# Carrying transposed gate/up blocks through DRAM, with a re-planned instruction order, in a macaron block with an RWKV-7 and pooling mixer

## The chip, the core and the metric

The kernel runs on one core of one Trainium2 chip. The metric is the time of one execution on the device in microseconds, the median of several runs. A core has five engines that run side by side, each working through its own instructions in order: TensorE (PE in the profile; its weight loads are PEld), VectorE (DVE), ScalarE (ACT), GpSimd (POOL) and SyncE (SP). SP computes nothing here; it issues most of the DMA transfers. An instruction whose inputs are not ready holds up everything behind it on its own engine, and this is true of SP's queue of transfers too.

## The reference

One block over 256 tokens of width 2048, in float32: a half-weighted SwiGLU feed-forward (FFN) of inner width 5632, a mixer, and a second such FFN.

```python
def _swiglu(x, w_gate, w_up, w_down):
    return (jax.nn.silu(x @ w_gate) * (x @ w_up)) @ w_down
...
def reference(x, ...):
    h = x
    for l in range(DEPTH):
        f = _swiglu(_rmsnorm(h, ln_ffn1_pre[l]), ffn1_gate[l], ffn1_up[l], ffn1_down[l])
        h = h + MACARON_WEIGHT * _rmsnorm(f, ln_ffn1_post[l])
        mx = _hybrid_mixer(_rmsnorm(h, ln_mix_pre[l]), ...)
        h = h + _rmsnorm(mx, ln_mix_post[l])
        f = _swiglu(_rmsnorm(h, ln_ffn2_pre[l]), ffn2_gate[l], ffn2_up[l], ffn2_down[l])
        h = h + MACARON_WEIGHT * _rmsnorm(f, ln_ffn2_post[l])
    return h
```

DEPTH is 1. The mixer multiplies by `w_in`, runs an RWKV-7 scan over 16 heads and a pooling branch, gates the two, and multiplies by `w_out`. The change concerns the hidden activations of the two FFNs, `silu(x @ w_gate) * (x @ w_up)`, on their way to the product with `w_down`, and the order of all instructions.

## The kernel before

**Products.** Every float32 matrix is split into a high part H (cast to fp32r) and a low part L (the rest), and a product is three passes on TensorE: H·H, H·L, L·H (`mm3`, line 510). Weights come from DRAM by SP into one of five raw buffers `w32` of 128x1024 floats (`raw`, line 466; 512 KB, which is two k of 128 rows by 512 columns). ACT casts a raw buffer to `wH`, VectorE subtracts to give `wL` (`split`, line 491); there are five buffers of each of these too (`WS_BUFS`). In the profile raw buffers are named w. A raw buffer is free for the next load when VectorE has made `wL`.

**FFN.** The inner width is worked through in 11 blocks of 512 columns (`ffn`, line 846). A block takes the gate columns (bank names f0, f1, for the two halves of 128 tokens) and the up columns (l0, l1), over 16 k of 128. Pairs of k may instead be done by a seven-product scheme (`early` and `late`, lines 732 and 751), called quads here: four products of a quad run within the block before (early), three in its own block (late). A quad takes its weights as six half loads into three raw buffers, and VectorE forms sums of them first. `GATE_QUADS` gives the quads of a block: none in blocks 0 and 1, three in 2 to 8, two in 9 and 10. `block_seq` (line 819) lays out a block: gate pairs with late quads between, then up pairs, with the next block's early quads put in at even distances.

**From a block to the down product.** At a block's end the activations lie with tokens on the partitions, but the down product wants the inner columns there. VectorE transposes 32x32 squares within the partitions into a tile `T1` (`turn`, line 659; named T in the profile). What is left is to exchange 32-partition groups, since a transpose of 128x128 moves the square (i, q) to (q, i). `carry` (line 664) does this by 16 DMA transfers on SP from `T1` to another tile `x32` (named x), each 32 partitions by 256 columns, 32 KB. Then ACT casts x to a high part and VectorE subtracts for the low part, two halves each (named xH, xL); they are `hT`, which the down product reads only after all 11 blocks. There are two FFNs, so 22 carries and 352 such transfers.

**Mixer and stage borders.** `gemm_tok` with `lead` (line 516) is used for the first product after a norm (mixer and second FFN): it loads `STAG` k of weights and does the first half of the tokens for these before the second half, so that TensorE has work while the second half is still being normalised and transposed. With `trail` it does the last 16 k of a stage half by half (`by_half`, line 550); there the weights of the first `STAG` k use the five rotating buffers, and those of the rest are held in units, the pool of 33 tiles of 128x1024 floats (`NUNITS`) which all activations share.

**What sets the order.** Nothing is issued directly. Every call is recorded as an `Op`, and `Plan` works out the order for all engines by simulating them (`simulate`, line 237), then emits it (`emit`, line 369). Since `emit` makes all instructions at line 391, the profile gives L391 for every one of them, and groups are told apart by the tiles' names. Planned costs come from `cost` (line 185): a transfer occupies SP's queue for 370 ns, and moves at 387 GB/s or less for short rows. In the simulation a transfer's data moves no earlier than 1900 ns after its issue and after the transfers before it; it counts as landed 300 ns after that. `deadlines` (line 218) gives each op a due time from its users, a DMA 2000 ns earlier; of the ready ops of an engine, the one due first goes first. An op off TensorE may be taken only when its nominal time is at most `AHEAD` ns, 25,000, past where TensorE's main stream stands. On the chip each engine keeps the planned order, whatever the real times are, and waits where the inputs of the next one aren't there.

Of the kernel before, what the change touches and what calls it, by code (L numbers as in the profile page):

```python
# [19 lines left out]
P = 128  # L20
# [15 lines left out]
W32_BUFS = 5  # L36
WS_BUFS = 5
NUNITS = 33
STAG = 10
TRAIL = 16  # L40
WARM = 12
TB = 6
AHEAD = 25000.0
EASE = 2.0
GATE_QUADS = [0, 0] + [3] * 7 + [2, 2]
DOWN_QUADS = ((8, 1, 2.4), (8, 1, 1.7))
# [17 lines left out]
class Engine:  # L64

    def __init__(s, plan, key, real):
        s.plan, s.key, s.real = plan, key, real
# [4 lines left out]


SYNC = 55.0
TABLES = {AF.Exp: (0,), AF.Sigmoid: (2,), AF.Tanh: (0, 2, 18), AF.Silu: (18,)}
IN_ORDER = ("w32", "wH", "wL", "hH", "hL")


class Plan:
# [105 lines left out]
    def cost(s, o, name, w, r, k):  # L185
        psum = any(getattr(s.tiles.get(x.tensor.name), "psum", False) for x in w + r)
        size = lambda ap: math.prod(ap.shape[1:]) if len(ap.shape) > 1 else 1
        n = max([size(x) for x in w + r] or [0])
        o.tab, o.nbytes = None, 0
        if name == "dma_start":  # L190
            x = w[0]
            o.nbytes = math.prod(x.shape) * 4
            run = min(min(y.shape[-1] for y in w + r) * 4, 2048)
            o.dur = o.nbytes / (387.0 if run >= 2048 else 387.0 * max(run, 64) * 1.25
                                / (run + 512))
            o.pace = {"SP": 370.0, "ACT": 110.0, "POOL": 600.0}[o.eng]
            return
        if o.eng == "PE":
            c = size(w[0])
            slow = name == "matmul" and r[0].dtype == F32  # L200
            o.pace = 2 * (0.7 * c + 32) / 2.4 if slow else (c + 32) / 2.4
            o.dur = o.pace + 165
        elif o.eng == "ACT":
            extra = 90.0 * sum(isinstance(k.get(x), bass.AP) for x in ("scale", "bias"))
            extra += 100.0 if "accum_out" in k else 0.0
            o.tab = TABLES.get(k.get("func"))
            o.pace, o.dur = n / 1.2 + 103 + extra, n / 1.2 + 200 + extra
        elif o.eng == "DVE":
            f = 1 / 0.96
            if name in ("tensor_copy", "tensor_scalar") and not psum:  # L210
                f /= 2
            more = 45.0 if name == "scalar_tensor_tensor" else 26.0 if name == "transpose" \
                else 0.0
            o.pace, o.dur = n * f + 75 + more, n * f + 158 + more
        else:
            o.pace = o.dur = n * 1.0 + 110

    def deadlines(s):
        for o in s.ops:
            for p in o.preds:  # L220
                s.ops[p].succs.append(o)
        soon = {}
        for o in s.ops:
            if o.stream == "chain":
                soon[o.i] = max([soon[q] + s.ops[q].dur + SYNC for q in o.preds if q in soon
                                 and s.ops[q].nom == o.nom] or [0.0])
        for o in reversed(s.ops):
            d = o.nom + (0.0 if o.eng == "PE" else o.lag) + soon.get(o.i, 0.0) * EASE
            for x in o.succs:
                if o.eng == "PE" and x.eng == "PE":  # L230
                    continue
                e = x.dl - o.dur - SYNC - (2000 if o.nbytes else 0)
                if e < d:
                    d = e
            o.dl = d

    def simulate(s):
# [18 lines left out]
        events, now, done, dma, tab = [], 0.0, 0, 0.0, None  # L256
        out, rel = [], itertools.count()
# [11 lines left out]
        def go(o):  # L269
            nonlocal done, dma, tab, prog  # L270
            e = o.eng
            if o.stream == "main" and e == "PE":
                prog = o.nom
            o.start = now
            for i in o.new:
                if i.slot is None:
                    i.slot = slots[i.tag].popleft()
                    turn[i.tag] += 1
            pace, dur = o.pace, o.dur
            if o.tab and tab not in o.tab:  # L280
                tab = o.tab[0]
                pace, dur = pace + 1300, dur + 1300
            free[e] = now + pace
            if o.nbytes:
                dma = max(now + 1900, dma) + o.dur
                o.end = dma + 300
            else:
                o.end = now + dur
            done += 1
            out.append(o)  # L290
            heapq.heappush(events, (free[e], next(rel), None))
            for i in o.tiles:
                i.left -= 1
                i.dl = max(getattr(i, "dl", 0.0), o.end)
                if not i.left and i.tag in s.tags:
                    heapq.heappush(events, (i.dl + SYNC, next(rel), i))
            for x in o.succs:
                t = now if e == "PE" and x.eng == "PE" else o.end + SYNC
                if x.stream == "chain" and x.eng == "PE" and e != "PE":
                    t += 250  # L300
                x.ready = max(x.ready, t)
                x.left -= 1
                if not x.left:
                    heapq.heappush(wait[x.eng], (x.ready, x.i))
                    heapq.heappush(events, (x.ready, next(rel), None))
        while done < len(ops):
            moved = True
            while moved:
                moved = False
                for e in engines:  # L310
# [3 lines left out]
                    while w and w[0][0] <= now:  # L314
                        _, i = heapq.heappop(w)
# [3 lines left out]
                    g = gate[e]  # L319
                    while g and g[0][0] <= prog + AHEAD:  # L320
                        i = heapq.heappop(g)[1]
                        heapq.heappush(av, (ops[i].dl, i))
                    if e == "PE":
                        for st in rank:
                            q = streams[st]
                            if q and ready[q[0].i] and can(q[0]):
                                go(q.popleft())
                                moved = True
                                break
                        continue  # L330
                    skipped = []
                    while av:
                        d, i = heapq.heappop(av)
                        if can(ops[i]):
                            go(ops[i])
                            moved = True
                            break
                        skipped.append((d, i))
# [8 lines left out]
            while events and events[0][0] <= now:  # L347
                _, _, i = heapq.heappop(events)
# [56 lines left out]
class Block:  # L405
    def __init__(s, tc, ctx):
        s.tc = tc
        s.real = real = tc.nc
        E = ctx.enter_context
        s.n = 0  # L410
        s.after = []
        s.cp = E(tc.tile_pool(name="cp", bufs=1))
        s.wp = E(tc.tile_pool(name="wp", bufs=1))
        s.up = E(tc.tile_pool(name="up", bufs=1))
        s.tp = E(tc.tile_pool(name="tp", bufs=1))
        s.sp = E(tc.tile_pool(name="sp", bufs=1))
        s.dp = E(tc.tile_pool(name="dp", bufs=1, space=bass.MemoryType.DRAM))
        s.pm = E(tc.tile_pool(name="pm", bufs=1, space=PSUM))
        s.pt = E(tc.tile_pool(name="pt", bufs=1, space=PSUM))
        s.nc = s.plan = Plan(tc)  # L420
        s.ident = s.const([P, P], "ident")
        make_identity(real, s.ident)
        s.mhalf = s.const([P, 16], "mhalf")
        real.gpsimd.memset(s.mhalf, -0.5)
# [91 lines left out]
    def gemm_tok(s, w, c0, at, KT, evac, lead=False, trail=False, xs=None):  # L516
# [11 lines left out]
        def both(k0, k1):  # L528
            for k2 in range(k0, k1, 2):
                keep(s.load_w(w, k2, min(2, k1 - k2), c0, 512))  # L530
                for k in range(k2, min(k2 + 2, k1)):
                    do(k, 0)
                    do(k, 1)
# [9 lines left out]
        elif lead:  # L543
            s.by_half(w, c0, 0, STAG, do, keep)
            k0 = STAG
        both(k0, KT)
# [3 lines left out]
    def by_half(s, w, c0, k0, k1, do, keep, done=None):  # L550
        for k in range(k0, k1, 2):
            keep(s.load_w(w, k, 2, c0, 512, k - k0 >= STAG))
        for h in range(2):
# [110 lines left out]
    def carry(s, T1, T):  # L664
        nc = s.nc
        x = s.unit((P, 1024), F32, "x32")
        for i in range(4):
            for q in range(4):
                nc.sync.dma_start(out=x[q * 32:q * 32 + 32, i * 256:i * 256 + 256],
                                  in_=T1[i * 32:i * 32 + 32, q * 256:q * 256 + 256])  # L670
        v = x.rearrange("p (i h k t) -> p k h i t", i=4, h=2, k=4)
        T.extend(s.new_T(1))
        for h in range(2):
            H, L = [t.rearrange("p k (h i t) -> p k h i t", h=2, i=4)[:, :, h] for t in T[-1]]
            s.split(v[:, :, h], H, L)
# [1099 lines left out]
```

## Time and profile before

| | us |
|---|---|
| median of 3 runs (lowest, highest) | 2149.8 (2149.71, 2152.92) |
| the profiled execution, its own time | 2155.24 |
| its span, first to last instruction | 2153.5 |
| VectorE / ScalarE busy | 1669.6 / 1141.9 |
| queue 1 (SP's transfers), share of 16 DMA engines | 60.4% |
| mean traffic over the span | 207 GB/s |

The stages of the span: the first FFN's gate and up blocks until about 520 us, its down product until 755, the mixer until about 1413, the second FFN from there, with its down product from about 1915.

How to read it: times are microseconds from the first instruction, unless marked ns. Engine names with a q (SPq) mean an engine's queue of issued transfers. A group `out<-in` names tiles with their buffer numbers left out. A timeline row gives start, duration, engine, line, operation, tiles, a count of merged instructions, and in brackets the idle time of the engine before it with what ended it. TensorE is pipelined: a product of 512 columns is shown as 0.39 us long, but the next starts 0.227 us later when nothing holds it up, so its busy share overstates its use. A row of waits gives engine and tile, what it waited for, the sum, the count and the longest. A row of windows gives the stretch and its length, and the busy time of each engine with its instruction count.

### The profile page before, as it was taken

Reading aid. Unit: us, or ns where it says so; the run is one execution under the profiler, and the core shown is the slowest. Engines: PE = TensorE matmul, PEld = TensorE weight load, DVE = VectorE, ACT = ScalarE, POOL = GpSimd, SP = SyncE. Lnnn points to the kernel's source line nnn. Section 1 sums busy time; section 2 is a strip of 40 time slices with the busy share of each in tenths; the row PEclk is TensorE's granted clock in tenths of the full one; section 3 lists DMA queues with packets and bytes.
Section 4 is the critical chain, followed back from the end, with each engine's and each line's share of the span. In section 5 each row is a group of like instructions: output and inputs, shape, how many; then the busy total and the mean of one; then the engine's idle time right before and its main releaser. Section 6 shows DMA issues by size and latency. Waiting matters only on the chain.

```text
span 2153.5 us, 30194 instructions
## 1 busy us (share of the span) xinstructions
PE 2076.4 (96%) x10847; PEld 1724.4 (80%) x10847; DVE 1669.6 (78%) x2176; ACT 1141.9 (53%) x1520; POOL 74.8 (3%) x146
## 2 busy tenths in 40 slices
PE   9899999999999999999999999999999999999998
PEld 7777777788778889978987788877777777878786
DVE  7888878777979765798768756588887887679795
ACT  7555555554546564664556344465554564455453
POOL 1000000000000020001200110010000000000000
PEclk9999999999999999999999999999999999999999
DMA  7666677766657566536465475566666776666574
GB/s 265 195 225 226 203 239 243 233 218 195 213 190 265 200 208 199 152 112 207 121 210 159 138 254 182 189 207 222 226 212 227 244 244 218 203 208 214 194 260 141
DMA packets 258047, 444.85 MB, mean 207 GB/s; under 512 B 23007, under 2 KB 70249, under 8 KB 257897
## 3 DMA queue, kind: packets, MB, share of 16 engines
q1 hardware_dynamic: 251721, 422.47, 60.4%
q0 software_dynamic: 5888, 19.93, 2.7%
q8 instruction: 85, 1.39, 0.3%
q10 hardware_dynamic: 288, 0.52, 0.1%
q14 instruction: 65, 0.53, 0.1%
HBM read 422.91 MB, written 8.39 MB: 200 GB/s over the span
## 4 chain that ended last, share of the span: by engine, by line
PE 47%; DVE 18%; issue 12%; SPq 11%; DMA 8%; ACT 3%; POOL 0%; DVEq 0%; ACTq 0%; POOLq 0%
PE l L391 14%; SPq L391 11%; PE f L391 9%; PE mm L391 9%; DVE wL L391 9%; PE mc L391 8%; DMA w<-in_ffn_gate_dram 5%; PE p L391 3%; ACT wH L391 2%; DVE t L391 2%; DVE w L391 1%; DVE sg L391 1%; DMA w<-in_ffn_up_dram 1%; DMA w<-in_ffn_down_dram 1%; DVE pr L391 1%
## 5 line engine op out<-in xcount | busy, mean ns | idle before, releaser
L391 ACT CAST wH<-w 128x1024 fp32r<-128x1024 f32 (+2 forms) x725 | 748.4, 1044 | 666.3 <-DVE w L391 158.8
L391 DVE TENSOR_TENSOR wL<-w,wH 128x1024 fp32r<-128x1024 f32 (+2 forms) x725 | 867.4, 1207 | 233.1 <-ACT wH L391 230.8
L391 PE MATMUL l<-wL,xH 128*128 128x512 f32 x772 | 303.9, 394 | 12.2 <-DVE wL L391 12.2
L391 PE MATMUL l<-wH,xH 128*128 128x512 f32 x772 | 303.3, 393 | 10.8 <-ACT wH L391 10.8
L391 PE MATMUL l<-wH,xL 128*128 128x512 f32 x772 | 301.7, 391 | 0.0
L391 PE MATMUL f<-wL,xH 128*128 128x512 f32 x664 | 261.2, 393 | 14.8 <-DVE wL L391 14.8
L391 PE MATMUL f<-wH,xH 128*128 128x512 f32 x664 | 260.1, 392 | 1.3 <-ACT wH L391 1.3
L391 PE MATMUL f<-wH,xL 128*128 128x512 f32 x664 | 259.7, 391 | 0.0
L391 PE MATMUL mm<-wL,xH 128*128 128x512 f32 x500 | 198.7, 397 | 3.0 <-DVE wL L391 3.0
L391 PE MATMUL mm<-wH,xH 128*128 128x512 f32 x500 | 197.3, 395 | 0.0
L391 PE MATMUL mm<-wH,xL 128*128 128x512 f32 x500 | 197.2, 394 | 0.0
L391 PEld LDWEIGHTS l<-wL,xH 128*128 128x128 f32 x772 | 145.6, 189 | 47.5 <-DVE wL L391 17.9
L391 PEld LDWEIGHTS l<-wH,xH 128*128 128x128 f32 x772 | 145.7, 189 | 47.0 <-ACT wH L391 17.1
L391 DVE TENSOR_TENSOR t<-w,w 128x1024 f32<-128x1024 f32 (+1 forms) x132 | 134.5, 1019 | 53.0 <-DMA w<-in_ffn_gate_dram 34.6
L391 PEld LDWEIGHTS l<-wH,xL 128*128 128x128 f32 x772 | 145.8, 189 | 29.6
L391 PEld LDWEIGHTS f<-wL,xH 128*128 128x128 f32 x664 | 125.5, 189 | 45.7 <-DVE wL L391 19.8
L391 PE MATMUL mc<-xH,wL 128*128 128x256 f32 x560 | 159.3, 284 | 1.1 <-DVE wL L391 1.1
L391 PE MATMUL mc<-xL,wH 128*128 128x256 f32 x560 | 159.8, 285 | 0.0
L391 PE MATMUL mc<-xH,wH 128*128 128x256 f32 x560 | 159.0, 284 | 0.0
L391 PEld LDWEIGHTS f<-wH,xH 128*128 128x128 f32 x664 | 125.5, 189 | 29.6 <-ACT wH L391 3.0
L391 PEld LDWEIGHTS f<-wH,xL 128*128 128x128 f32 x664 | 125.4, 189 | 25.7
L391 PEld LDWEIGHTS mm<-wL,xH 128*128 128x128 f32 x500 | 94.5, 189 | 23.8 <-DVE wL L391 4.3
(320 smaller groups left out, 3090.5 us busy)
## 6 DMA issues: line engine op xcount, KB each, us to landing
w<-in_w_in_dram SPq DMA_DIRECT2D x128, 512.0 KB, 3.9
w<-in_ffn_up_dram SPq DMA_DIRECT2D x126, 512.0 KB, 4.7
w<-in_ffn_gate_dram SPq DMA_DIRECT2D x124, 512.0 KB, 4.5
w<-in_ffn_down_dram SPq DMA_DIRECT2D x112, 512.0 KB, 4.8
w<-in_ffn_gate_dram SPq DMA_DIRECT2D x154, 256.0 KB, 4.2
w<-in_ffn_up_dram SPq DMA_DIRECT2D x150, 256.0 KB, 4.4
w<-in_ffn_down_dram SPq DMA_DIRECT2D x128, 256.0 KB, 4.0
w<-in_w_out_dram SPq DMA_DIRECT2D x32, 512.0 KB, 3.4
```

The costliest lines, as they stand in the source:

```text
L391: ins = o.fn(*[real(x) for x in o.a], **{n: real(x) for n, x in o.k.items()})
```

## The change

`carry` writes `T1` whole to a DRAM tile of its own (128x1024 floats, 512 KB) in one transfer, and reads it back by four transfers, one for each group of 32 destination partitions; each takes four runs of 256 floats per partition (128 KB in all). All five are issued by SP. The reads need the write to have landed.

In the plan's model, a transfer on SP takes 500 ns of its queue, not 370; it counts as landed 1600 ns after its data has moved (`LAND`), not 300; its due time lies 2500 ns before its users', not 2000. `AHEAD` goes from 25,000 to 40,000 ns, and `STAG` from 10 to 8. The order of the whole program is planned anew with these.

```diff
-STAG = 10
+STAG = 8
...
-AHEAD = 25000.0
+AHEAD = 40000.0
...
 SYNC = 55.0
+LAND = 1600.0
...
-            o.pace = {"SP": 370.0, "ACT": 110.0, "POOL": 600.0}[o.eng]
+            o.pace = {"SP": 500.0, "ACT": 110.0, "POOL": 600.0}[o.eng]
...
-                e = x.dl - o.dur - SYNC - (2000 if o.nbytes else 0)
+                e = x.dl - o.dur - SYNC - (2500 if o.nbytes else 0)
...
-                o.end = dma + 300
+                o.end = dma + LAND
...
+        s.cx = itertools.count()
...
     def carry(s, T1, T):
         nc = s.nc
         x = s.unit((P, 1024), F32, "x32")
-        for i in range(4):
-            for q in range(4):
-                nc.sync.dma_start(out=x[q * 32:q * 32 + 32, i * 256:i * 256 + 256],
-                                  in_=T1[i * 32:i * 32 + 32, q * 256:q * 256 + 256])
+        d = s.dram((P, 1024), f"cx{next(s.cx)}")
+        nc.sync.dma_start(out=d, in_=T1)
+        for q in range(4):
+            nc.sync.dma_start(
+                out=x[q * 32:q * 32 + 32].rearrange("s (i c) -> s i c", i=4),
+                in_=d.rearrange("(i s) (q c) -> q s i c", i=4, q=4)[q])
```

## The prediction

> **What bounds the kernel now.** I read the page first, then the queue of SP, then TensorE beside it.
>
> ```profile
> PE 2076.4 (96%) x10847; PEld 1724.4 (80%) x10847; DVE 1669.6 (78%) x2176; ACT 1141.9 (53%) x1520; POOL 74.8 (3%) x146
> PE 47%; DVE 18%; issue 12%; SPq 11%; DMA 8%; ACT 3%; POOL 0%; DVEq 0%; ACTq 0%; POOLq 0%
> x<-T SPq DMA_DIRECT2D x352, 32.0 KB, 1.8
> L391 SPq DMA_DIRECT2D x<-T x352: 507/589/1715, 60.4 to 1923.1; - x176
> ```
>
> TensorE looks full, yet only 47% of the chain that ended last runs through it; 11% runs through SP's queue, which computes nothing. The transfers of this change are the 352 named x<-T (22 blocks of 16). Each holds SP's queue for 589 ns (the middle of min/median/max), so sixteen take 9.4 us, though each lands 1.8 us after its issue. The timeline of SP's queue shows them as bursts:
>
> ```profile
> 60.45 10.09 SPq L391 DMA_DIRECT2D x<-T  x16
> ...
> 212.63 0.43 SPq L391 DMA_DIRECT2D w<-in_ffn_up_dram  x1
> 213.18 10.01 SPq L391 DMA_DIRECT2D x<-T  x16
> 223.29 0.53 SPq L391 DMA_DIRECT2D w<-in_ffn_gate_dram  x1
> ...
> 394.74 11.09 SPq L391 DMA_DIRECT2D x<-T  x16
> ...
> 439.06 10.24 SPq L391 DMA_DIRECT2D x<-T  x16
> ...
> 481.02 10.02 SPq L391 DMA_DIRECT2D x<-T  x16
> ...
> 1461.23 10.24 SPq L391 DMA_DIRECT2D x<-T  x16
> ...
> 1874.45 10.02 SPq L391 DMA_DIRECT2D x<-T  x16
> ```
>
> For 10 us no weight is asked for. Six to fourteen microseconds after the end of the burst of 213.18 TensorE runs dry; in brackets stands its idle time and who ended it:
>
> ```profile
> 229.31 0.50 PE L391 MATMUL f<-wL,sH 128*128 128x512 f32 x1 [0.27 <-DVE wL L391]
> ...
> 231.77 0.50 PE L391 MATMUL f<-wH,xH 128*128 128x512 f32 x1 [0.35 <-ACT wH L391]
> 233.03 0.50 PE L391 MATMUL f<-wL,xH 128*128 128x512 f32 x1 [0.76 <-DVE wL L391]
> ...
> 236.38 0.49 PE L391 MATMUL l<-wH,xH 128*128 128x512 f32 x1 [0.56 <-ACT wH L391]
> 237.64 0.50 PE L391 MATMUL l<-wL,xH 128*128 128x512 f32 x1 [0.77 <-DVE wL L391]
> ```
>
> The chain of waits over 205 to 240 us goes the same way, through the burst, then this late weight transfer, then its two casts:
>
> ```profile
> by line: SPq L391 31.8%; DVE wL L391 23.2%; DMA w<-in_ffn_gate_dram 17.7%; issue 10.5%; PE f L391 6.1%; ACT wH L391 6.0%; DVE sg L391 2.0%; DVE w L391 1.9%; DVE t L391 1.7%; DVE hL L391 1.7%; DVE T L391 0.4%; ACTq L391 0.1%
> ...
> 224.39 6.18 DMA w<-in_ffn_gate_dram
> ```
>
> **What the bursts cost.** A run without a gap gives the price of one product of 512 columns, from the chain of waits over the whole span:
>
> ```profile
> 603.96 27.89 PE l L391 x123
> ```
>
> 27.89/123 = 0.2268 us. The code gives the products from the first burst of an FFN (end of block 0) to its tenth (end of block 9). Block 1: 16 k x 2 tensors x 2 halves x 3 = 192, and 36 of the next block's three early quads. Blocks 2 to 7: 120 standard, 27 late, 36 early, 183 each. Block 8: 171; block 9: 186. Together 1683, or 381.6 us. The bursts stand 481.02 - 60.45 = 420.6 us apart in the first FFN and 1874.45 - 1461.23 = 413.2 in the second. Lost: 39.0 + 31.6 = 70.6 us over 18 blocks, **3.9 us a burst**. Part of it is a lower clock after the longest stops:
>
> ```profile
> 392.00:437.00 45.00, 40.41 (x165) 32.62 (x164) 33.43 (x38) 22.31 (x27) 0.00 (x0) 0.92 0.66 216
> ...
> 208.00:254.00 46.00, 43.30 (x186) 34.44 (x185) 37.28 (x43) 24.17 (x29) 0.00 (x0) 1.00 0.70 230
> ...
> 70.00:116.00 46.00, 39.88 (x165) 32.81 (x166) 37.08 (x39) 23.12 (x27) 0.00 (x0) 0.93 0.78 254
> ```
>
> (PE, PEld, DVE and ACT busy; then granted clock, DMA share, GB/s.) The floor can be reached: block 9, from 439.06 to 481.02, took 42.0 us for 186 x 0.2268 = 42.2, although a burst stood in it. The block before took 44.3 for 38.8.
>
> Why 3.9 and not 10: a block of 183 products (41.5 us) uses up 19 raw weight buffers, one each 2.18 us; the five there are last 10.9 us, and a new load lands after 4.7 (row below), which leaves 6.2 us of cover. 10.1 - 6.2 = 3.9, the loss found another way. I use this rule from here on: **a hold of SP beyond 6.2 us is lost**.
>
> **Part one, the transfers.** Removed: sixteen issues, 10.1 us of queue with their gaps. Added: one issue of 512 KB to DRAM, four of 128 KB back, and one wait, that of the reads for the write. None of the added ones is in the trace; the nearest rows:
>
> ```profile
> L391 SPq DMA_DIRECT2D out_dram<-fg x8: 332/332/364, 2137.1 to 2150.0; - x8
> DMA to landing us min/median/max: 2.4/2.4/2.4
> ...
> w<-in_ffn_up_dram SPq DMA_DIRECT2D x126, 512.0 KB, 4.7
> msp<-sgb POOLq DMA_DIRECT2D x8, 256.0 KB, 3.0
> ...
> L391 SPq DMA_DIRECT2D w<-in_ffn_down_dram x240: 327/378/1533, 498.5 to 2120.0; - x120
> DMA to landing us min/median/max: 3.0/4.4/9.0
> ```
>
> Issue of the write: 0.33 (a store of SP) to 0.38; I take 0.4 with its gap. A read: 0.33 to 0.59 (it fills 32 partitions, as x<-T does); near the latter, 0.55, so 2.2, and 0.2 of gaps. Hold without a wait: 2.8 us. The wait: the write lands 2.4 (an idle queue) to 9.0 us after its issue (the longest load), most likely about 4.7, as loads of its size on the same queue do. The plan reckons 1.9 + 524288/387000 + 1.6 = 4.85 us before it puts the reads into SP's order, so weight loads stand between and the wait is 0 to 1 us; behind it on SP stand only weight loads. Hold: 2.8 to 3.8 us, under the cover. If the reads stood right behind the write, it would be 2.8 + 4.7 = 7.5.
>
> The Trainium skill (DMA: Bandwidth & Descriptors, section "Issuing engines are not separate DMA queues") says that a sequencer's time to start a DMA is usually small beside the DMA. By that rule the burst costs next to nothing and the sum is 0. The rows disagree here: 589 ns each, sixteen times, with weights behind them.
>
> The block is needed only in the down product, so a later arrival costs nothing there. It adds 0.5 MB of traffic a block. 230 GB/s at a share of 0.70 is 329 GB/s, so 1.6 us of DMA; in blocks of 42 us the share becomes 0.70 x 46/42 + 1.6/42 = 0.80. A share of 0.78 is seen above. Value 0; if it all lengthened landings, the cover would fall to 4.6, still over 3.8.
>
> **Part two, later landings in the plan.** The plan reckoned 16 x 0.37 = 5.9 us for a burst that took 10.1, 4.2 too few. ACT's cast of the block stands in an order made by that, and waits with its weights behind it:
>
> ```profile
> ACT xH L391 <- DMA x<-T: 96.9, 21, 7.3
> SPq L391 <- DVE wL L391: 1031.0, 527, 15.9
> ```
>
> 96.9/21 = 4.6 us, those 4.2. With five transfers at 500 ns and 1.6 us more for landing, plan and rows agree. This delay is the same one that TensorE sees, so I don't count it twice; left as it is it would cost up to 4.6 a block. SP idles 1031 us in all waiting for free buffers, so slower issues in the plan (500 against 378) starve nothing.
>
> **Part three, look ahead and STAG.** They move work at stage borders and in the mixer. TensorE's waits there:
>
> ```profile
> 760.97 0.50 PE L391 MATMUL mm<-wL,xH 128*128 128x512 f32 x1 [0.71 <-DVE wL L391]
> ...
> 938.75 0.50 PE L391 MATMUL mm<-wL,xH 128*128 128x512 f32 x1 [1.60 <-DVE wL L391]
> 943.74 0.48 PE L391 MATMUL pA<-AR,BK 64*128 64x128 f32 x2 [1.96 <-DVE BK L391]
> ...
> 1205.49 1.98 PE L391 MATMUL pM<-T,X 32*32 32x32 f32 x64 [1.75 <-DVE T L391]
> ```
>
> STAG 8 keeps one of five split buffers free at two borders (gains at most 2 x 0.71) and gives the second half's preparation 6 products less, 2 x 1.36 us at worst. Of the look ahead I know only the size of what it can move: these waits, 6 us together, gone or doubled. Value 0 for both, bounds -8 and +9.
>
> **Sum.** Hold 3.8 is under 6.2, so the rule says all 70.6 us. I leave a fifth, 14 us, because VectorE becomes tight: 37.28 us busy in a block that is to last 41.5, 90%, and its work bunches at the block's end. Gain 56.5. The profiled execution took 2155.2 us (span 2153.5), so 2098.7; the median of the runs is 5.4 lower: **2093 us**.
>
> **Rivals.** (1) *The wait takes the burst's place in part.* The reads come at the queue's head with the write not landed: hold 7.5 us, 1.3 beyond the cover, 23 us over 18 blocks, beside the 14: gain 33, **2116**. Reads as long as the longest x<-T (1.7 us each) give the same. For it: a load after the burst took 6.18 us. Against it: the plan's 4.85. (2) *Slower: the write lands late.* It sits behind weight loads on a fuller queue; SP, in order, stands at the first read and no weight is asked for. It decides from a landing of 10.1 - 2.8 = 7.3 us; at the 9.0 of the longest load the hold is 11.8, 1.7 more than now, 37 us over 22 blocks: **2187**. Against it: 9.0 is a maximum, the median 4.4, and loads placed between the two eat part of the wait. (3) *The burst was hidden anyway*, and VectorE's own loop paces the blocks: **2150**, as the skill's rule has it. For it: block 9, at its floor with a burst. Against it: the chain's 31.8% through SP and stops that follow each burst.
>
> **How the numbers follow.** Forecast 0.70, (1) 0.15, (2) 0.10, (3) 0.05. The forecast's own range: all 70.6 and 8 more, 2071, to 28 left and 9 lost, 2116. To hold eight in ten the range takes in (1) with some of its spread: 2068 to 2132; (2) and (3) stay out. 0.2%, 4.3 us, is what a measurement can tell. Faster 0.85, same 0.05, slower 0.10.
>
> **What would show it.** After: 22 writes and 88 reads of x on SP, under 4 us of queue a block; tenth burst 385 to 392 us after the first in each FFN; ACT's waits for x under 30 us in all; SPq under 5% of the chain. Wrong if SP waits for the new DRAM tile's landing by more than 3 us a block (1, 2), if the blocks stay at 45 us without bursts (3), or if TensorE's waits in the mixer grow by more than 9 us.

## The result and the profile after

The changed kernel takes 2077.2 us (median of 4 runs, 2075.8 to 2079.2) where the kernel before took 2151.0 beside it (median of 4): a ratio of 0.966 (95% interval 0.964 to 0.967). The profiled execution took 2076.1 us, 79.1 less than the one before. Predicted were 2093, in a range of 2068 to 2132.

Busy time by engine, and the chain of waits by engine, from the page of the kernel after:

```profile
PE 2044.1 (99%) x10847; PEld 1718.3 (83%) x10847; DVE 1670.5 (81%) x2176; ACT 1148.3 (55%) x1518; POOL 82.4 (4%) x146
PE 79%; DVE 9%; issue 8%; ACT 2%; POOL 1%; DMA 1%; SPq 0%; DVEq 0%; POOLq 0%; ACTq 0%
```

The work is the same (10847 instructions on TensorE, 2176 on VectorE). What is new is what the end waits for: TensorE carries 79% of the chain, not 47%, and SP's queue nothing, not 11%. A part of the gain is clock: the mean granted clock of the profiled execution rose from 0.990 to 0.996, by my estimate 0.006 x 2074, or 12 us of the 79.

The new transfers by their tiles (nanoseconds of queue time, min/median/max); the line at which the plan is emitted is L392 now, and L395 in some runs below:

```profile
L392 SPq DMA_DIRECT2D x<-cx x88: 326/423/1285, 63.4 to 1841.8; - x88
L392 SPq DMA_DIRECT2D cx<-T x22: 326/327/342, 59.6 to 1837.0; - x22
```

One block's stretch of SP's timeline:

```profile
195.01 0.33 SPq L392 DMA_DIRECT2D cx<-T  x1
196.08 0.33 SPq L392 DMA_DIRECT2D w<-in_ffn_gate_dram  x1
196.46 0.44 SPq L392 DMA_DIRECT2D w<-in_ffn_up_dram  x1
198.00 0.33 SPq L392 DMA_DIRECT2D w<-in_ffn_gate_dram  x1
198.38 0.42 SPq L392 DMA_DIRECT2D w<-in_ffn_up_dram  x1
198.91 1.79 SPq L392 DMA_DIRECT2D x<-cx  x4
```

Write and reads hold the queue 0.33 + 1.79 = 2.1 us, and four weight loads stand between them. The write's landing is hidden behind those, as the waits show (sum, times, longest):

```profile
SPq L392 <- DVE T L392: 73.7, 22, 7.6
...
SPq L392 <- DMA cx<-T: 0.8, 2, 0.4
...
ACT xH L392 <- DMA x<-cx: 12.0, 10, 3.3
```

SP does stand still ahead of each write, until VectorE has made T: 73.7/22 = 3.4 us a carry, which the holds below leave out. In the block shown it cost nothing: the weight load behind the write had to wait once more for a raw buffer, from 195.34 to 196.08, so there was none that SP could have filled earlier.

The first and the tenth carry of each FFN in SP's timeline:

```profile
59.57 0.34 SPq L392 DMA_DIRECT2D cx<-T  x1
...
441.77 0.34 SPq L392 DMA_DIRECT2D cx<-T  x1
...
1419.17 0.34 SPq L392 DMA_DIRECT2D cx<-T  x1
...
1800.17 0.34 SPq L392 DMA_DIRECT2D cx<-T  x1
```

And the window of one block between two carries (PE, PEld, DVE, ACT and POOL busy, clock, DMA share, GB/s):

```profile
195.00:236.40 41.40, 41.40 (x184) 34.31 (x183) 37.10 (x42) 24.34 (x29) 0.00 (x0) 1.00 0.82 267
```

Nine blocks take 382.2 and 381.0 us; their 1683 products need 381.6. **The gate and up stage now runs at TensorE's floor**: no idle time at all in the block shown, at full clock. By the same marks the 79.2 us of span come from: the nine blocks 38.4 and 32.2, together 70.6; from the tenth carry to the end of the span 279.05 - 274.13 = 4.9 in the second FFN; the remaining 3.7 nearly all in the first FFN, before its first carry (60.45 - 59.57 = 0.9) and behind its tenth (2.6, worked out below).

### The profile page after: what moved, and what is told of

It is laid out like the page before. It is cut to its first block, busy times and chain, and to the rows that moved or that the text cites. A ratio compares the mean times of both kernels' runs of the same rounds, so it can differ in the third digit from the quotient of the medians.

```text
span 2074.3 us, 29823 instructions
## 1 busy us (share of the span) xinstructions
PE 2044.1 (99%) x10847; PEld 1718.3 (83%) x10847; DVE 1670.5 (81%) x2176; ACT 1148.3 (55%) x1518; POOL 82.4 (4%) x146
## 4 chain that ended last, share of the span: by engine, by line
PE 79%; DVE 9%; issue 8%; ACT 2%; POOL 1%; DMA 1%; SPq 0%; DVEq 0%; POOLq 0%; ACTq 0%
PE l L392 30%; PE f L392 26%; PE mm L392 9%; PE mc L392 7%; PE p L392 4%; DVE wL L392 3%; DVE xL L392 1%; DVE pr L392 1%; DVE fg L392 1%; DVE Z L392 1%; POOL rs L392 1%; ACT junk L392 0%; PE pY L392 0%; ACT xH L392 0%; ACT wH L392 0%
## 5 line engine op out<-in xcount | busy, mean ns | idle before, releaser
L392 ACT CAST wH<-w 128x1024 fp32r<-128x1024 f32 (+2 forms) x722 | 746.9, 1044 | 628.2 <-PE l L392 143.7
L392 DVE TENSOR_TENSOR wL<-w,wH 128x1024 fp32r<-128x1024 f32 (+2 forms) x722 | 866.0, 1209 | 254.4 <-ACT wH L392 251.6
L392 PE MATMUL l<-wL,xH 128*128 128x512 f32 x764 | 297.5, 389 | 0.8 <-DVE wL L392 0.8
L392 PE MATMUL l<-wH,xH 128*128 128x512 f32 x764 | 297.4, 389 | 0.0
L392 PE MATMUL l<-wH,xL 128*128 128x512 f32 x764 | 297.2, 389 | 0.0
L392 PE MATMUL f<-wH,xL 128*128 128x512 f32 x664 | 258.3, 389 | 0.0
L392 PE MATMUL f<-wH,xH 128*128 128x512 f32 x664 | 258.3, 389 | 0.0
L392 PE MATMUL f<-wL,xH 128*128 128x512 f32 x664 | 258.3, 389 | 0.0
L392 PE MATMUL mm<-wL,xH 128*128 128x512 f32 x496 | 196.6, 396 | 0.0
L392 PE MATMUL mm<-wH,xH 128*128 128x512 f32 x496 | 196.5, 396 | 0.0
L392 PE MATMUL mm<-wH,xL 128*128 128x512 f32 x496 | 196.3, 396 | 0.0
L392 PEld LDWEIGHTS l<-wL,xH 128*128 128x128 f32 x764 | 143.4, 188 | 30.7 <-DVE wL L392 1.1
L392 PEld LDWEIGHTS l<-wH,xH 128*128 128x128 f32 x764 | 143.4, 188 | 29.8
L392 PEld LDWEIGHTS l<-wH,xL 128*128 128x128 f32 x764 | 143.4, 188 | 29.7
L392 PE MATMUL mc<-xH,wL 128*128 128x256 f32 x560 | 159.8, 285 | 1.3 <-DVE wL L392 1.3
L392 PE MATMUL mc<-xL,wH 128*128 128x256 f32 x560 | 159.9, 286 | 0.0
L392 PE MATMUL mc<-xH,wH 128*128 128x256 f32 x560 | 159.7, 285 | 0.0
L392 DVE TENSOR_TENSOR t<-w,w 128x1024 f32<-128x1024 f32 (+1 forms) x132 | 134.6, 1020 | 17.8 <-DMA w<-in_ffn_down_dram 10.3
L392 PEld LDWEIGHTS f<-wL,xH 128*128 128x128 f32 x664 | 124.6, 188 | 25.9
L392 PEld LDWEIGHTS f<-wH,xL 128*128 128x128 f32 x664 | 124.6, 188 | 25.9
L392 PEld LDWEIGHTS f<-wH,xH 128*128 128x128 f32 x664 | 124.6, 188 | 25.9
L392 ACT CAST wH<-t 128x1024 fp32r<-128x1024 f32 x82 | 86.1, 1050 | 53.7 <-DVE t L392 27.1
```

Of the source, the lines that this page charges most:

```text
L392: ins = o.fn(*[real(x) for x in o.a], **{n: real(x) for n, x in o.k.items()})
```

## The experiments

Each kernel ran beside the kernel before on the same chip, which took 2151.9 us beside e1 to e4, 2152.2 beside e5 to e8 and 2154.3 beside e9 to e12. The kernel after was not run again beside them, so a difference of a few microseconds from its 2077.2 says little. Short names: H, an unbroken hold of SP's queue beyond its cover is lost; the rivals are in the texts quoted.

**1. The carry alone (e1_carry_only).** The kernel after with the old constants:

```diff
-STAG = 8
+STAG = 10
...
-AHEAD = 40000.0
+AHEAD = 25000.0
...
-LAND = 1600.0
+LAND = 300.0
...
-            o.pace = {"SP": 500.0, "ACT": 110.0, "POOL": 600.0}[o.eng]
+            o.pace = {"SP": 370.0, "ACT": 110.0, "POOL": 600.0}[o.eng]
...
-                e = x.dl - o.dur - SYNC - (2500 if o.nbytes else 0)
+                e = x.dl - o.dur - SYNC - (2000 if o.nbytes else 0)
```

> The new carry (one write, four reads) under the old plan (370 ns, landing 300, due 2000, AHEAD 25000, STAG 10). Theory H (an unbroken hold of SP's queue beyond a cover of 6.2 us is what was lost): the hold falls to 2.8 us and a wait of 0 to 2, so nearly all is won: 2085 us (2075 to 2105), blocks near 41.5 us. Rival P (the re-planned order won it: ACT's cast of x no longer stands too early): most of the loss stays, 2125 or more, with ACT's wait for x still about 4 us a block.

2079.8 us, 0.967 (0.965 to 0.969). Nearly the whole gain, with the interval of the whole change overlapping. And ACT still waits for the block:

```profile
ACT xH L392 <- DMA x<-cx: 39.0, 21, 3.7
SPq L392 <- DMA cx<-T: 5.9, 5, 1.9
```

39.0/21 = 1.9 us a block on ACT, 5.9 us in all on SP for the write's landing; neither shows in the time beyond the 2.6 us by which it differs from the kernel after.

**2. The plan alone (e2_plan_only).** The kernel after with the old sixteen transfers in `carry`.

> The new plan with the old sixteen transfers on SP, which stay one after another. H: the hold stays 10 us and 3.9 us a burst stay lost: 2145 us (2130 to 2155). P: 2110 or less, ACT's wait for x near 1 us a block.

2139.6 us, 0.995 (0.992 to 0.997). ACT's waits for x halve against the kernel before, by its row of waits:

```profile
ACT xH L392 <- DMA x<-T: 45.5, 20, 7.3
```

The bursts on SP stay, and so does most of the loss; by the page's chain of waits SP still carries 5%:

```profile
PE 60%; DVE 15%; issue 10%; DMA 7%; SPq 5%; ACT 3%; POOL 1%; DVEq 0%; ACTq 0%; POOLq 0%
```

Rival P, that the order won it, falls with these two.

**3. Sixteen transfers, spread (e3_spread16).** The old transfers in the new plan, not due until later:

```diff
-                    s.carry(T1[0], hT)
+                    with s.set(lag=45000.0):
+                        s.carry(T1[0], hT)
```

> The new plan with the old sixteen transfers, but their due time (and that of the casts behind them) is 45 us, not 12, after the block: in the order for SP they come in groups of at most four with weight loads between. No DRAM, the same 22 x 10 us of queue time in all. H: no hold is over 2.5 us, so 2080 us (2070 to 2095). Rival Q (the sum of SP's queue time or the number of transfers is what costs): 2130 or more.

2097.6 us, 0.976 (0.973 to 0.978): a little over 2095, the end of what H gave, and far from Q's 2130. From the second to the ninth carry of each FFN the groups are of at most four, as in this one in SP's timeline:

```profile
205.70 1.78 SPq L392 DMA_DIRECT2D x<-T  x3
207.58 0.53 SPq L392 DMA_DIRECT2D w<-in_ffn_gate_dram  x1
208.16 0.43 SPq L392 DMA_DIRECT2D w<-in_ffn_up_dram  x1
208.63 2.42 SPq L392 DMA_DIRECT2D x<-T  x4
211.15 0.53 SPq L392 DMA_DIRECT2D w<-in_ffn_gate_dram  x1
211.72 1.77 SPq L392 DMA_DIRECT2D x<-T  x3
```

But the first carry of all was hardly spread. Thirteen of its transfers stand unbroken on SP, and behind them TensorE has one stop:

```profile
65.60 8.19 SPq L392 DMA_DIRECT2D x<-T  x13
```

```profile
84.17 0.79 PE L392 MATMUL l<-wH,xH 128*128 128x512 f32 x1 [3.87 <-ACT wH L392]
```

The same window in this run and in the kernel after:

```profile
61.00:120.00 59.00, 54.66 (x230) 44.42 (x229) 47.25 (x55) 27.85 (x32) 0.00 (x0) 0.94 0.70 222
```

```profile
61.00:120.00 59.00, 58.25 (x258) 47.89 (x257) 52.39 (x60) 31.45 (x36) 0.00 (x0) 1.00 0.83 262
```

It makes 28 products fewer there, 28 x 0.2268 = 6 us. The tenth and eleventh carries, and the first of the second FFN, have groups of five and six.

The same 352 transfers, with DRAM untouched, lose 20 us, not 74, when weight loads pass between most of them. 6 of the 20 fall into the window behind the hold that was left at the first carry; where the other 14 come from is open. ACT's waits within 160 to 420 us are a candidate, since its casts of x come where the last group has only just been issued:

```profile
ACT xH L392 <- DMA x<-T: 27.3, 5, 6.6
```

But e1 and e12 below bear such waits at no cost, and it was not tried by itself.

**4, 5, 9. A hold of chosen length (e4_hold16, e5_hold6, e9_hold11).** The kernel after, with n more transfers of 32 KB from `T1` to a DRAM tile that nothing reads, put directly behind the write in SP's order (n = 16, 6, 11):

```diff
+        order = [x for o in order if o.i not in away for x in [o] + s.behind.get(o.i, [])]
...
-        nc.sync.dma_start(out=d, in_=T1)
+        first = nc.sync.dma_start(out=d, in_=T1)
+        e = s.dram((P, 1024), f"ex{next(s.cx)}")
+        s.plan.behind[first.i] = [
+            nc.sync.dma_start(out=e[j // 4 * 32:j // 4 * 32 + 32, j % 4 * 256:j % 4 * 256 + 256],
+                              in_=T1[j // 4 * 32:j // 4 * 32 + 32, j % 4 * 256:j % 4 * 256 + 256])
+            for j in range(n)]
```

> The kernel after, and directly behind each write to DRAM sixteen more transfers of 32 KB from T1 to a DRAM tile that nothing reads, unbroken on SP. H: a hold of 5.7 us (at 0.33 each) to 10.5 (at 0.6); at 10.5 it loses 4.3 us a block, 86 us over 20 blocks, 2160 us; at 5.7 nothing, 2080; between, by the rule: loss = hold - 6.2 in every block. P and a theory in which only transfers that somebody waits for cost: 2085 or less.

> As the run with sixteen more transfers behind the write, but six. SP is held about 3.3 us by the write and these, and 2.3 by the reads soon after, 5.6 in all. H with a cover of 6.2 us: no loss, 2077 us (2070 to 2085). H with the cover that the run with sixteen gives (5.5 us lost a block at 8.1 + 2.3 = 10.4 of hold, so 4.9): 0.7 a block, 2091. Rival L (each more transfer costs its share, with no cover): 6/16 of the 97 us, 2113.

> Eleven more transfers behind the write: a hold of 0.4 + 11 x 0.48 = 5.7 us and 2.3 for the reads, 8.0. The run with six (5.6) lost nothing, the one with sixteen (10.4) 5.5 us a block. H with a cover of 4.9: 3.1 a block, 62 us over 20 blocks, 2139 us. With the 6.2 of the prediction: 1.8 a block, 2113. If the loss starts only near 8 (cover counted without the reads, which have weight loads around them): 2085.

2174.1 us (1.012, 1.009 to 1.014), 2082.6 (0.968, 0.966 to 0.970) and 2113.7 (0.981, 0.979 to 0.983). SP's timeline of e4, of e5 and of e9, one block each:

```profile
214.66 0.33 SPq L395 DMA_DIRECT2D cx<-T  x1
215.03 7.73 SPq L395 DMA_DIRECT2D ex<-T  x16
...
224.69 0.43 SPq L395 DMA_DIRECT2D x<-cx  x1
...
225.64 1.75 SPq L395 DMA_DIRECT2D x<-cx  x3
```

```profile
237.71 0.33 SPq L395 DMA_DIRECT2D cx<-T  x1
238.08 3.09 SPq L395 DMA_DIRECT2D ex<-T  x6
...
243.10 1.86 SPq L395 DMA_DIRECT2D x<-cx  x4
```

```profile
245.89 0.33 SPq L395 DMA_DIRECT2D cx<-T  x1
246.26 5.64 SPq L395 DMA_DIRECT2D ex<-T  x11
...
253.84 1.85 SPq L395 DMA_DIRECT2D x<-cx  x4
```

| more transfers | hold, reads included, us | 22 x (hold - 6.2) | rule's time | measured |
|---|---|---|---|---|
| 0 | 2.1 | 0 | 2077 | 2077.2 |
| 6 | 3.5 + 1.9 = 5.3 | 0 | 2077 | 2082.6 |
| 11 | 6.0 + 1.9 = 7.9 | 37 | 2114 | 2113.7 |
| 16 | 8.1 + 2.2 = 10.3 | 90 | 2167 | 2174.1 |

The prediction's rule with its cover of 6.2 us holds within about 7 us over the whole range, if all 22 carries count; with the 20 of the texts quoted it gives 2110 and 2159, 15 short of e4. The four reads are counted into the hold, though four or five weight loads stand between them and the rest. As they are nearly the same in all three runs, these can't tell a cover of 6.2 with the reads from one of 4.3 without them; the kernel before can, since it has a hold of 10.1 and no reads, and at 4.3 it would have lost 128 us. A part of e4's loss is clock (0.987 granted, 0.996 in the kernel after, by my estimate 20 us), so the size of the cover is known to a microsecond or so, not better. L, a price for each transfer from the first on, would have put six at 2113. My estimate of a cover of 4.9, made from one block of e4, is refuted by e9.

**6, 7, 12. The same traffic from GpSimd's queue (e6_traffic16, e7_pool16, e12_pool_old_plan).** e6 is e4 with the sixteen further transfers issued by `nc.gpsimd`. e7 is the new plan with the old sixteen transfers from `T1` to x on `nc.gpsimd`. e12 is the kernel before with that one word changed:

```diff
-                nc.sync.dma_start(out=x[q * 32:q * 32 + 32, i * 256:i * 256 + 256],
+                nc.gpsimd.dma_start(out=x[q * 32:q * 32 + 32, i * 256:i * 256 + 256],
```

> The same sixteen more transfers from T1 to a DRAM tile that nothing reads, but issued on GpSimd's queue, so that SP isn't held. H: 2077 to 2087 us. Rival D (it is the load on the DMA engines and later landings that cost the 97 us, not SP's queue): 2140 or more.

> The new plan with the old sixteen transfers from T1 to x, issued on GpSimd's queue: no DRAM, sixteen small transfers, SP free. H: 2075 to 2090 us, about the kernel after. Rival D (the sixteen small transfers themselves, or their latency, cost): 2110 or more.

> The kernel before, with one word changed: its sixteen transfers are issued by GpSimd, not SP. Old plan, which takes 600 ns for each of these. H: SP's hold is gone, 2075 to 2090 us. Rival (the DRAM route or the new plan is needed for the last part): 2100 or more.

2080.8 us (0.967, 0.966 to 0.969), 2075.6 (0.965, 0.963 to 0.966) and 2076.5 (0.963, 0.962 to 0.965). Beside e4's 2174, e6 shows that the sixteen transfers cost 97 us on SP's queue and 3.6 on another: it is the queue, not the load on the DMA engines. And e12 gets the whole gain with no DRAM tile and no new plan. Its transfers by their tile, with their landing in us:

```profile
L391 POOL DMA_DIRECT2D x<-T x352: 498/498/675, 61.1 to 1848.5; - x176
DMA to landing us min/median/max: 1.6/3.6/6.1
```

They take 22 x 16 x 0.498 = 175 us of GpSimd's queue, where nothing else waits in these blocks. ACT's wait for x in the same run:

```profile
ACT xH L391 <- DMA x<-T: 38.7, 22, 6.2
```

**8, 10. VectorE's reserve (e8_dve4, e10_dve8).** Additions at the end of `carry` whose results nothing uses, n = 4 and 8:

```diff
+        for _ in range(n):
+            nc.vector.tensor_tensor(out=s.tmp("dz"), in0=T1[:, :512], in1=T1[:, 512:],
+                                    op=ALU.add)
```

> The kernel after, with four more additions of 128x512 on VectorE at the end of each block, 2.75 us a block, whose results nothing uses; VectorE goes from 37.2 of 41.5 us a block to 39.9, 96%. If VectorE was as tight at 90% as the prediction took it (a fifth of the loss left for that), the last 10% can't be had: 2.5 us a block lost, 2130 us. If its free time can be used to the full: 2077 to 2085.

> Eight more additions on VectorE a block, 37.2 + 8 x 0.55 (the run with four showed 39.4) = 41.6 us of VectorE in a block of 41.5: at its end. If VectorE bounds only where it is full: blocks 42 to 43 us, 2085 to 2110. If it has a reserve that the profile's busy time hides: 2083 or less.

2081.0 us (0.967, 0.966 to 0.969) and 2135.5 (0.991, 0.989 to 0.993). A window of e8 as long as a block, then one of e10 from carry to carry:

```profile
195.00:236.40 41.40, 41.40 (x184) 34.30 (x183) 39.39 (x45) 24.32 (x30) 0.00 (x0) 1.00 0.83 267
```

```profile
259.10:303.59 44.49, 42.03 (x185) 34.26 (x184) 41.97 (x50) 24.48 (x30) 0.00 (x0) 1.00 0.79 248
```

VectorE at 39.4 of 41.4 us, 95%, costs TensorE nothing in this window. At 42.0 the block takes 44.5, and from the second to the eighth carry of both FFNs blocks take 44.2 to 46.2: far more than the 0.6 by which 42.0 exceeds 41.4. In VectorE's timeline of this run the eight additions stand together, with one subtraction for wL between (in e8 they stand two and two):

```profile
215.34 1.89 DVE L392 TENSOR_TENSOR dz<-T 128x512 f32<-128x512 f32 x3
217.15 1.22 DVE L392 TENSOR_TENSOR wL<-w,wH 128x1024 fp32r<-128x1024 f32 x1
218.28 3.10 DVE L392 TENSOR_TENSOR dz<-T 128x512 f32<-128x512 f32 x5
```

And in SP's timeline no weight is issued for 5 us:

```profile
218.40 0.40 SPq L392 DMA_DIRECT2D w<-in_ffn_gate_dram  x1
223.68 0.35 SPq L392 DMA_DIRECT2D w<-in_ffn_up_dram  x1
```

SP waits 4.8 of these for a wL, which frees a raw buffer. A hold of VectorE thus reaches the same loop of buffers as a hold of SP. How much of the 58 us is that and how much the sheer sum was not separated; the expectation of 2110 at most was too low.

**11. STAG back to 10 (e11_stag10).**

> The kernel after with STAG 10 as before. After shows a new stop of TensorE of 2.3 us at the mixer's start, on the row sums' transposition. If STAG 8 brought it: 2072 to 2076 us. If the look ahead or the landings did: 2077 and above, and STAG is worth nothing either way.

2075.7 us, 0.963 (0.962 to 0.965). The timeline of TensorE after has one stop at the mixer's start that this run does not have:

```profile
727.33 0.33 PE L392 MATMUL rb<-ident,rb 128*128 128x128 f32 x1 [2.10 <-DVE rb L392]
```

So STAG 8 brought that stop. On the whole time the two can't be told apart, since their intervals overlap. The same holds for e7, e11, e12 and the kernel after: none of these beats it beyond its measurement.

## Why the prediction was right, and where it was off

**The burst as the cause** was right. e1 and e2 separate the two halves of the change, e4 and e6 the queue from the traffic, and e12 moves only the queue. That the loss is a hold less a cover of about 6 us is shown at three lengths by e5, e9 and e4. That this cover is five buffers' use less one landing was not tested: no run changed the buffers or the landing. So the close agreement of the two ways of finding 3.9 us a burst may be partly luck; over all 22 carries the measured loss is 79.1/22 = 3.6.

**The cost of the added parts** was right within its bounds: 0.33 for the write (0.4 taken), 0.45 for a read with its gap (0.55 taken), a wait of 0.8 us in the whole run (0 to 1 a block taken). The plan's 4.85 us was not needed to put weights between: under the old plan of e1, which reckons 1.3 us less, SP waits 5.9 us in all and at most 1.9 at once. So rival 1 had the mechanism but hardly any size, and rival 2, from a landing of 7.3 us on, never came near. The DMA share rose to 0.82, forecast 0.80, with no harm.

**The step that was mis-sized is the fifth of the loss left to VectorE.** "I leave a fifth, 14 us, because VectorE becomes tight: 37.28 us busy in a block that is to last 41.5, 90%" measured 0: the blocks stand at their floor with VectorE at 37.1 us, and e8 shows that even 39.4 leaves them there. The sum by the rule alone, 70.6, was exact. This is also why the tenth carry came 382.2 and 381.0 us after the first, ahead of the 385 to 392 named as a sign.

**A second term was left out.** The count went from the first burst to the tenth of each FFN. What the tenth and eleventh cost lies behind it. I put down to them the 4.9 us from the tenth to the end of the span in the second FFN. In the first, from the tenth carry to TensorE's first stop at the mixer (741.15 - 0.92 before, 699.35 - 0.98 after in TensorE's timeline), 259.2 became 256.6, 2.6 us less. 56.5 + 14.1 + 7.5 = 78.1 of the 79.1 us by which the profiled execution fell.

**Part two** was half right. The plan's 4.2 us too few for a burst fit ACT's 4.6 us, and the new plan of e2 halves that wait. But "left as it is it would cost up to 4.6 a block" is wrong: in e12 ACT waits 38.7 us and in e1 39.0, at the full gain, while e2, with 45.5, keeps most of the loss. So ACT's wait went along with TensorE's and was not its cause; whether waits as long as the 96.9 us before would cost anything without the burst was not tried. The new plan by itself won 12 us with the bursts there (e2 against before), and no more than can be measured without them (e1).

**Part three**, value 0, was right in sum: from TensorE's first stop at the mixer to the first carry of the second FFN, 1461.23 - 740.23 = 721.0 us became 1419.17 - 698.37 = 720.8. Its bound named the mixer's start, where the 2.1 us stop came, with 1.36 us for each border.

Rival 3, that the burst was hidden, leaned on the Trainium skill (DMA: Bandwidth & Descriptors, section "Issuing engines are not separate DMA queues"), by which spreading transfers over engines saves only issue time, usually small. The first half agrees with e7 and e12, and the second does not: the issue time taken off one queue was worth 78 us here (2154.3 to 2076.5 in e12). Block 9 before, at its floor with a burst in it, had looked like evidence for the rival; it was not, since the block before it, with a burst of its own, took 5.5 us more than its floor. Why block 9 lost nothing is not shown.

## What to carry to other kernels

Read an in-order queue of transfers as you would an engine: find its longest stretch with nothing useful in it, and compare that with the cover (estimated here as buffers times the time each lasts, less one landing). In this kernel a hold below the cover cost little or nothing, and beyond it about every microsecond was lost at every repetition. Before rebuilding such transfers, try to issue them from an engine that is idle there: one word did as much here as the new route and a new plan together. And an engine's waits for the late data are not a cause until a run shows the time falling with them.

## What the runs showed of the hardware that was not expected

The queue time of a transfer on SP did not follow its bytes. Medians: 327 ns for 512 KB from 128 partitions to DRAM (cx<-T), 423 for 128 KB from DRAM to 32 partitions (x<-cx), 589 for 32 KB between two tiles on the chip (x<-T before), and 420 for the same 32 KB to DRAM, in e4:

```profile
L395 SPq DMA_DIRECT2D ex<-T x352: 303/420/1913, 63.8 to 1938.7; - x176
```

So the smallest transfers, on-chip to on-chip, were the dearest to issue, 1.4 times those of the same size to DRAM. The length of the burst is not the reason: in e3 four in a group took 2.42 us, 0.6 each. On GpSimd's queue they took 498.
